# A two-layer block with experts: the loop for left-over tokens at the end, the first weights' loads, and the read of the record table

## The chip, the cores and the metric

The kernel runs on one core of a Trainium2 chip. The metric is the device time of one execution in microseconds (us). TensorE does the matrix products, VectorE (DVE), ScalarE (ACT) and GpSimd (POOL) the rest; DMA transfers are issued from the queues of SP, ScalarE and GpSimd.

## The reference, cut to what matters

There are 512 image tokens and 256 context tokens of 1024 numbers each. In both layers a mixer (three kinds of attention, joined by a gated product and `w_out`) is added to the tokens. Layer 0 does this for all 768 tokens, layer 1 for the 512 of the image alone. Then each token goes to two of 16 experts.

```python
for l in range(DEPTH):                                   # two layers
    h = rms_norm(x, g_norm1[l]) * (1.0 + sc1) + sh1
    y, yc = mixer_sublayer(h, hc, ...)
    x = x + gt1 * y
    h = rms_norm(x, g_norm2[l]) * (1.0 + sc2) + sh2
    ...
    scores = jax.nn.sigmoid(tokens @ w_router)           # 16 experts, the best two are used
    hid = jax.nn.silu(xb @ w_gate[e]) * (xb @ w_up[e])   # 1024 -> 512, for the tokens of expert e
    y = hid @ w_down[e]                                  # 512 -> 1024
    x = x + gt2 * out[:b * length].reshape(x.shape)
return rms_norm(x, g_final)
```

The scale and shift vectors (`sc1`, `sh1`, `gt1`, `sc2`, `sh2`, `gt2`) come from products of a condition vector with `w_mod`.

## The kernel before

**Weights.** All weights are read once, in a fixed order, in chunks of 512 KB (128 partitions of 1024 numbers), by SP's queue (`Weights.load`, L83). A load is written into the program as soon as a page of memory is free for it by the program's own count, up to a bound `ws.limit`, after which the loads wait until the bound is raised. A chunk is used raw, or it is split in two halves of its precision: ScalarE makes `wh` (L102), DVE makes `wl` (L114), and each product is three matmuls.

**Out phase.** `out_phase` multiplies the joined branches by `w_out`, one tile of 128 tokens after the other, six in layer 0 and four in layer 1. While TensorE is in tile m, the steps of the norm and the routing of tile m−1 or m−2 are hooked in between its products (`HOOKS`, `second`). The last tile has a class of its own (`Last`); its `end` stores the normed rows `h` for the gathers (L1539) and the tokens (L1540), both on SP's queue, and then raises the bound for the weights. The bound is 20 chunks into the experts' weights from the start of the phase, and 28 from there on. The pages of `w_out` come free during the last tile.

**Routing.** `Router.pair` works on two tiles at a time. TensorE gives the ranks of the tokens in their experts (`rk`), DVE compares (`oh`) and makes a row number for each place, and TensorE multiplies the comparisons with the tokens' numbers (`first`, L2168) so that the first 128 tokens of the experts 13, 14 and 15 are known at once. The last pair starts the gather of the first expert's rows (`x0`, L2173) as soon as its numbers are there. Then four indirect stores write records of token and weight to a table in memory (L2204). `finish` reads the table's part for these three experts on ScalarE's queue (`rec`, L2217), and `arrange` orders the other 13 experts.

**Experts.** `moe` works through 16 slots. The first three are the experts 13 to 15, whose weights (36 chunks) can be loaded before the routing is done; the experts of the 13 others are read by SP from the order table. A slot gathers its tokens' rows from memory, multiplies by gate, up and down, and its `finish` scatters the result with GpSimd (L1669), in layer 1 by adding to the tokens. Later slots use raw weights for 64 tokens.

**The loop.** Slots have a fixed number of places. Tokens above it are worked off in a hardware loop (`For_i`, L1949) over `nmore` rounds, a number that the routing gives; its body is `late_block`. It stands behind slot 10 in layer 0 and behind slot 13 in layer 1 (`LOOPAT`). All five engines read `nmore` and branch there.

**What follows the experts.** In layer 0 there come three groups of modulation products for layer 1 (`fillers`, matmuls into `modps`), and then the mixer of layer 1: it loads a tile of the tokens and of the experts' result (L623, L625), adds and norms them, and transposes them (`h1t`, L648). In layer 1 the final gain is loaded (`gf`, L1971), the four tiles of the tokens are read back (`cx`, L1975), normed and stored (L1979).

Of the kernel before, what the change touches and what calls it, by code (L numbers as in the profile page):

```python
# [10 lines left out]
BF16 = mybir.dt.bfloat16  # L11
I32 = mybir.dt.int32
AF = mybir.ActivationFunctionType
OP = mybir.AluOpType
# [4 lines left out]
NE = 16  # L19
# [4 lines left out]
PG1 = 14  # L24
MW = 8
EX = {0: 3, 1: 5}
LB = 1
RING = 10


# [122 lines left out]
def tile_dit(ctx, tc, a, out):  # L153
    nc = tc.nc
# [47 lines left out]
    h2d = {l: dram.tile([(6 - 2 * l) * 128, D], F32, name=f"h2d{l}") for l in range(2)}  # L202
# [56 lines left out]
    last_out = {}  # L259
# [73 lines left out]
    ws = Weights(nc, specs)  # L333
# [144 lines left out]
    def mod_row(pool, tag, l, j, v, name):  # L478
        t = pool.tile([128, D], F32, tag=tag, name=name)
        nc.sync.dma_start(t, bc(modd[l][j, v, :], D))  # L480
        return t
# [853 lines left out]
    def merge(l):  # L1335
# [4 lines left out]
        rt = st.enter_context(tc.tile_pool(name=f"rt{l}", bufs=1))  # L1340
# [87 lines left out]
        R = Router(tc, nc, rt, small, l, nm, tri, ones, br, oac_tile, tabd[l], h2d[l])  # L1428
# [13 lines left out]
        last = nm - 1  # L1442
# [33 lines left out]
        class Last:  # L1476
# [57 lines left out]
            def end(self):  # L1534
                j = 1 if last >= NIMG else 0
                self.norm()
                self.turn(1)
                nc.vector.scalar_tensor_tensor(self.h, self.u, self.r[:, 0:1], sh2[j], op0=OP.mult, op1=OP.add)
                nc.sync.dma_start(h2d[l][last * 128:(last + 1) * 128, :], self.h)  # L1539
                nc.sync.dma_start(xa[l][last], xo[last])  # L1540
                ws.limit = last_out[l] + NEXT[l]
                ws.load()
                self.score(1)
                s = sg_of(last)
                nc.vector.scalar_tensor_tensor(s, self.lo[:, 0:NE], self.r[:, 0:1], self.shw, op0=OP.mult, op1=OP.add)
                nc.scalar.activation(s, s, AF.Sigmoid)
# [14 lines left out]
        def out_phase():  # L1561
# [6 lines left out]
            mod_rows(0)  # L1568
            load_x(0)
            load_x(1)  # L1570
            ws.limit = last_out[l] + FIRST[l]
            ws.load()
            steps = {}

# [52 lines left out]
            x0 = pool0.tile([128, D], F32, tag="pg", name=f"x0{l}")  # L1627
# [11 lines left out]
    def moe(l, R, late, ex, x0):  # L1639
# [217 lines left out]
        def next_fetch():  # L1857
            if queue:
                queue.pop(0).fetch()
# [11 lines left out]
        ws.low()  # L1871
        for _ in range(XG[l]):
            next_fetch()
        ws.limit = first_in + NEAR if l == 0 else len(ws.specs)
        ws.load()
        for s in range(AHEAD, NE):
# [46 lines left out]
        for s in range(NE):  # L1923
            nx = s + 1 < NE
            if nx:
                for b in blocks[s + 1]:
                    b.turn()
                    ahead()
            up = products(s, "u")
            gate(s, 0, 4, up, lambda i: blocks[s][i].times(up[i]))  # L1930
            if nx:
                gp = products(s + 1, "g")
                gate(s + 1, 0, HIDAT, gp)
            for b in blocks[s]:
                b.hidden()
            if nx:
                gate(s + 1, HIDAT, 4, gp)
                silus(s + 1, gp)
            for b in blocks[s]:
                b.sums()  # L1940
            for k in range(4):
                chunk(blocks[s], k, lambda i, c, w: blocks[s][i].down(*w, c))
            if l == 0 and not nx:
                ws.pump(4 * len(TURN) + WEND)
            ws.low()
            for b in blocks[s]:
                b.finish()
            if s == LOOPAT[l]:
                with tc.For_i(0, nc.values_load(R.nmore[0:1, 0:1], min_val=0, max_val=SLOTS)) as j:  # L1949
                    late_block(j)  # L1950
            if l == 0 and s == NE - 2:
                for j in range(2):
                    gt2.append(mod_row(pool0, "pg", 0, j, 5, f"gt2{j}"))
        if l == 0:
            for _ in fillers(TURN, pool0, "pg", held):
                pass
# [35 lines left out]
AHEAD = 3  # L1992
# [2 lines left out]
HT = {0: 2, 1: 1}  # L1995
TROWS = 896
MORE = 6
LOOPAT = {0: 10, 1: 13}
YO = {0: 2, 1: 1}
XG = {0: 2, 1: 1}  # L2000
NS = NE - AHEAD
SLOTS = 14
# [7 lines left out]
MPG = 4  # L2010
HIDAT = 2
YT = (0, 2)
HOOKS = {(0, 0): 1, (0, 4): 1, (0, 5): 2, (1, 1): 1, (1, 5): 1, (1, 7): 1}
LEAD = 3
FIRST = {0: 20, 1: 20}
NEXT = {0: 28, 1: 28}


def of_kind(l, kind):
# [18 lines left out]
class Router:  # L2038
# [77 lines left out]
    def pair(self, m, s, x0=None):  # L2116
# [42 lines left out]

        f = w[:, 15, :, 0:AHEAD]  # L2160
        stt(f, r2[:, :, NS:NE], 1.0, bb[:, :, NS:NE], op0=OP.add, op1=OP.mult)
        psf = self.oac_tile(f"first{l}_{m}")
        shape = [128, 2, 128]
        for e in range(AHEAD):
            oh = rt.tile(shape, BF16, tag="oh", name=f"oh{l}_{m}{e}", bufs=2)
            tt(oh, self.places[:, None, :].to_broadcast(shape), f[:, :, e:e + 1].to_broadcast(shape), op=OP.is_equal)
            for i in range(4):
                nc.tensor.matmul(psf[:, e:e + 1], oh[:, i // 2, :], self.idc[:, i % 2, m + i // 2:m + i // 2 + 1],  # L2168
                                 start=i == 0, stop=i == 3)
            if x0 is not None:  # L2170
                tt(self.first[:, e:e + 1], self.firstf[:, e:e + 1], psf[:, e:e + 1], op=OP.add)
                if e == 0:
                    nc.gpsimd.indirect_dma_start(  # L2173
                        out=x0, out_offset=None, in_=self.h2d,
                        in_offset=bass.IndirectOffsetOnAxis(ap=self.first[:, 0:1], axis=0))

                    tt(self.cum[:, m + 1, :], bb[:, 0, :], bb[:, 1, :], op=OP.add)
                    tt(self.cum[:, m + 2, :], self.cum[:, m, :], self.cum[:, m + 1, :], op=OP.add)
        if x0 is None:
            tt(self.firstf, self.firstf, psf[:, 0:AHEAD], op=OP.add)  # L2180
            tt(self.cum[:, m + 1, :], bb[:, 0, :], bb[:, 1, :], op=OP.add)
            tt(self.cum[:, m + 2, :], self.cum[:, m, :], self.cum[:, m + 1, :], op=OP.add)
        row = w[:, 14]
        stt(row, r2, float(NE), self.eidx[:, None, :].to_broadcast([128, 2, NE]), op0=OP.mult, op1=OP.add)
        four = [128, 2, 2, NE]
# [15 lines left out]
        for j in range(2):  # L2201
            for k in range(2):
                nc.gpsimd.memset(self.spacer, 0.0)
                st = nc.gpsimd.indirect_dma_start(  # L2204
                    out=self.tabd, out_offset=bass.IndirectOffsetOnAxis(ap=self.idx[:, m + j, k:k + 1], axis=0),
                    in_=self.recs[:, m + j, k, :], in_offset=None)
                for o in self.scat:
                    self.tc.declare_no_dep(st.ins, o.ins, reason="each record has a row of its own")
                self.scat.append(st)
        yield  # L2210

    def finish(self):

        nc, nt = self.nc, self.nt
        ps = self.oac_tile(f"cnt{self.l}")
        nc.tensor.matmul(ps[:, 0:NE], self.ones, self.cum[:, nt, :], start=True, stop=True)
        nc.scalar.dma_start(self.rec.rearrange("p e f -> p (e f)"),  # L2217
                            self.tabd.rearrange("(s e) f -> s (e f)", e=NE)[0:128, 4 * NS:4 * NE])
        self.arrange(ps[:, 0:NE])

    def record(self, out, at):
        self.nc.gpsimd.indirect_dma_start(
# [181 lines left out]
```

## Time and profile before

| | |
|---|---|
| time, median of 3 runs | 3008.33 us (3006.95 to 3015.96) |
| the profiled execution | 3013.33 us |
| its span | 3011.5 us |
| granted clock of TensorE, mean | 0.963 |
| TensorE busy | 2788.7 us, 93% |
| VectorE, ScalarE, GpSimd busy | 61%, 42%, 12% |
| DMA, mean over the span | 185 GB/s |

A share is an average over stages that differ. The page's 40 slices show it for DMA: its busy share is two or three tenths in the attention of both layers and nine tenths or more in three slices of each expert stage.

### The profile page before, as it was taken

What the parts mean: (1) busy time and instruction counts of PE and PEld (TensorE: products, weight loads), DVE (VectorE), ACT (ScalarE), POOL (GpSimd) and SP (SyncE); (2) the same over time, 40 slices, a digit from 0 to 9 for tenths busy, and PEclk for the clock granted to TensorE, in tenths of its full rate; (3) what the DMA queues carried; (4) which work ended last, traced back from release to release, by engine and by line L of the source; (5) the groups of instructions that cost most, each with busy time, mean ns of one, the idle gap of its engine ahead of it and who ended that gap; (6) DMA issues with size and microseconds to landing.
All of it is one profiled execution on the core that took longest, in us unless ns stands there. A gap on an engine that the chain in (4) does not pass through costs nothing. (4 is left out here: it accounts for less than half of the span.)

```text
span 3011.5 us, 42058 instructions
## 1 busy us (share of the span) xinstructions
PE 2788.7 (93%) x15253; PEld 2235.7 (74%) x15253; DVE 1822.4 (61%) x3235; ACT 1279.0 (42%) x2376; POOL 363.3 (12%) x425
## 2 busy tenths in 40 slices
PE   7999999999999999969999699999999999969983
PEld 4788888888888667757766478878888877757651
DVE  4675567676554455658665666667775645657441
ACT  4444445455443211227655454444554442226330
POOL 1220000000011000022221231000000100022211
PEclk8999999999999999979999899999999999979996
DMA  6333222222333666669998732232234456769995
GB/s 237 130 110 101 88 76 95 87 81 87 130 131 105 238 252 240 238 218 341 347 362 292 251 115 95 74 105 69 93 103 140 149 198 232 270 218 380 369 376 183
DMA packets 203989, 557.63 MB, mean 185 GB/s; under 512 B 27238, under 2 KB 51942, under 8 KB 203776
## 3 DMA queue, kind: packets, MB, share of 16 engines
q1 hardware_dynamic: 175968, 503.64, 46.6%
q0 software_dynamic: 10688, 25.02, 3.4%
q10 hardware_dynamic: 17120, 26.23, 2.4%
q8 instruction: 121, 1.98, 0.3%
q14 instruction: 92, 0.75, 0.1%
HBM read 461.95 MB, written 96.77 MB: 186 GB/s over the span
## 5 line engine op out<-in xcount | busy, mean ns | idle before, releaser
L114 DVE TENSOR_TENSOR wl<-raw,wh 128x1024 fp32r<-128x1024 f32 x474 | 565.2, 1221 | 150.5 <-ACT wh L102 140.3
L102 ACT CAST wh<-raw 128x1024 fp32r<-128x1024 f32 x474 | 484.7, 1050 | 365.4 <-DMA raw<-oT 122.1
L892 ACT ACTIVATE P<-sc,st 128x768 f32<-128x768 f32 (+4 forms) x240 | 176.2, 734 | 340.5 <-DVE st L890 213.9
L890 DVE TENSOR_REDUCE st<-sc 128x1 f32<-128x768 f32 (+4 forms) x240 | 178.6, 744 | 118.9 <-PE sc L179 113.3
L179 PE MATMUL psb<-wl,wh 128*128 128x512 f32 x480 | 189.7, 395 | 6.9 <-DVE wl L114 6.6
L926 ACT CAST ptH<-pt 128x512 fp32r<-128x512 f32 x264 | 142.9, 591 | 124.1 <-PE pt L911 103.6
L179 PE MATMUL psb<-wh,wh 128*128 128x512 f32 x480 | 192.9, 402 | 1.5 <-ACT wh L102 1.5
L179 PE MATMUL psb<-wh,wl 128*128 128x512 f32 x480 | 189.1, 394 | 2.0 <-DVE wl L114 2.0
L936 DVE TENSOR_TENSOR ptL<-pt,ptH 128x512 fp32r<-128x512 f32 x264 | 169.6, 682 | 9.3 <-ACT ptH L926 7.3
L911 PE MATMUL pt<-ident,P 128*128 128x128 f32 x1056 | 141.4, 275 | 14.2 <-ACT P L892 11.3
L911 PEld LDWEIGHTS pt<-ident,P 128*128 128x128 f32 x1056 | 119.7, 140 | 44.8 <-ACT P L892 31.0
L179 PE MATMUL psR<-wh,hH 128*128 128x512 f32 (+1 forms) x384 | 150.7, 392 | 0.0
L179 PE MATMUL psR<-wl,hH 128*128 128x512 f32 (+1 forms) x384 | 147.2, 383 | 2.7 <-DVE wl L114 2.7
L179 PE MATMUL psR<-wh,hL 128*128 128x512 f32 (+1 forms) x384 | 147.6, 384 | 0.0
L898 DVE TENSOR_SCALAR P<-P,st 128x768 f32<-128x768 f32 (+3 forms) x240 | 130.0, 542 | 8.5
L179 PEld LDWEIGHTS psb<-wh,wh 128*128 128x128 f32 x480 | 90.9, 189 | 46.8 <-issue 18.7
L486 POOL TENSOR_SCALAR rstd<-ss 128x4 f32<-128x4 f32 (+2 forms) x70 | 21.6, 309 | 830.6 <-ACT h L492 359.6
L179 PEld LDWEIGHTS psb<-wl,wh 128*128 128x128 f32 x480 | 91.1, 190 | 28.4 <-DVE wl L114 10.8
L179 PE MATMUL sc<-swkT,swqs 128*128 128x256 f32 x704 | 109.1, 281 | 2.2 <-ACT P L892 2.2
L179 PEld LDWEIGHTS psb<-wh,wl 128*128 128x128 f32 x480 | 91.0, 190 | 23.2 <-DVE wl L114 4.0
L179 PE MATMUL yps<-wh,hidT 128*128 128x512 f32 x320 | 105.0, 399 | 0.0
L1099 DVE COPY sc<-sink 128x1 f32<-128x1 f32 x160 | 25.8, 161 | 128.7 <-PE sc L179 122.5
(529 smaller groups left out, 6937.6 us busy)
## 6 DMA issues: line engine op xcount, KB each, us to landing
raw<-in_w_in_dram SPq DMA_DIRECT2D x136, 512.0 KB
raw<-in_w_gate_dram SPq DMA_DIRECT2D x128, 512.0 KB
raw<-in_w_up_dram SPq DMA_DIRECT2D x128, 512.0 KB
raw<-in_w_down_dram SPq DMA_DIRECT2D x128, 512.0 KB
raw<-in_w_mod_dram SPq DMA_DIRECT2D x96, 512.0 KB
raw<-in_w_br_dram SPq DMA_DIRECT2D x48, 512.0 KB
raw<-oT SPq DMA_DIRECT2D x30, 512.0 KB
raw<-in_w_out_dram SPq DMA_DIRECT2D x16, 512.0 KB
```

The source lines that it names most:

```text
L102: self.nc.scalar.copy(c.h, c.raw)
L114: self.nc.vector.tensor_tensor(c.l, c.raw, c.h.bitcast(F32), op=OP.subtract)
L179: nc.tensor.matmul(ps, lhs, rhs, start=start, stop=stop, skip_group_check=share)
L486: nc.gpsimd.tensor_scalar(r[:, 0:cnt], ss, four / n, four * EPS, op0=OP.mult, op1=OP.add)
L890: nc.vector.reduce_max(st[:, 1, h:h + 1], s[:, 0:self.ns], axis=AX.X, negate=True)
L892: nc.scalar.activation(self.P[h][:, 0:self.ns], s[:, 0:self.ns], AF.Exp, bias=st[:, 1, h:h + 1], accum_out=st[:, 2, h:h + 1])
L898: nc.vector.tensor_scalar(self.P[h][:, 0:self.nk], self.P[h][:, 0:self.nk], st[:, 3, h:h + 1], None, op0=OP.mult)
L911: nc.tensor.transpose(pt[:, c * 256 + h * 128:c * 256 + (h + 1) * 128], self.P[2 * x + h][:, i * 128:(i + 1) * 128], ident)
L926: nc.scalar.copy(ph, src)
L936: nc.vector.tensor_tensor(pl, src, ph.bitcast(F32), op=OP.subtract)
L1099: nc.vector.tensor_copy(s[:, nk:nk + 1], sink[:, hd:hd + 1])
```

## The change

There are four parts.

- The loop stands behind the last slot in both layers, before the modulation products in layer 0 and before the final gain's load in layer 1. `LB`, the number of buffers of tiles in the loop's body, is 2 instead of 1.
- The bound on weight loads is 36 chunks from the start of the out phase; it is not raised in `Last.end`. The store of the last tile's `h` goes by ScalarE's queue.
- The read of the record table leaves `finish` and becomes `R.load`, issued from GpSimd's queue after the first gathers of the experts' rows.
- In `pair`, for all but the last pair, the comparisons are done in the old place and the products `first` with their sum are moved behind the record stores, into a step of their own; `HOOKS` has one more entry for it. In the last pair the sum over the counts (`add_up`) comes behind the three products. `oh` is one tile of three instead of three from two buffers.

```diff
-LB = 1
+LB = 2
...
                 nc.vector.scalar_tensor_tensor(self.h, self.u, self.r[:, 0:1], sh2[j], op0=OP.mult, op1=OP.add)
-                nc.sync.dma_start(h2d[l][last * 128:(last + 1) * 128, :], self.h)
+                nc.scalar.dma_start(h2d[l][last * 128:(last + 1) * 128, :], self.h)
                 nc.sync.dma_start(xa[l][last], xo[last])
-                ws.limit = last_out[l] + NEXT[l]
-                ws.load()
...
-            ws.limit = last_out[l] + FIRST[l]
+            ws.limit = last_out[l] + 12 * AHEAD
             ws.load()
...
         for _ in range(XG[l]):
             next_fetch()
+        R.load()
         ws.limit = first_in + NEAR if l == 0 else len(ws.specs)
...
-            if s == LOOPAT[l]:
-                with tc.For_i(0, nc.values_load(R.nmore[0:1, 0:1], min_val=0, max_val=SLOTS)) as j:
-                    late_block(j)
             if l == 0 and s == NE - 2:
                 for j in range(2):
                     gt2.append(mod_row(pool0, "pg", 0, j, 5, f"gt2{j}"))
+        with tc.For_i(0, nc.values_load(R.nmore[0:1, 0:1], min_val=0, max_val=SLOTS)) as j:
+            late_block(j)
         if l == 0:
             for _ in fillers(TURN, pool0, "pg", held):
...
-LOOPAT = {0: 10, 1: 13}
...
-HOOKS = {(0, 0): 1, (0, 4): 1, (0, 5): 2, (1, 1): 1, (1, 5): 1, (1, 7): 1}
+HOOKS = {(0, 0): 1, (0, 4): 1, (0, 5): 2, (1, 1): 1, (1, 3): 2, (1, 5): 1, (1, 7): 1}
...
-FIRST = {0: 20, 1: 20}
-NEXT = {0: 28, 1: 28}
...
-        psf = self.oac_tile(f"first{l}_{m}")
...
+        oh = rt.tile([128, AHEAD, 2, 128], BF16, tag="oh", name=f"oh{l}_{m}")
+
+        def places(e):
+            tt(oh[:, e], self.places[:, None, :].to_broadcast(shape), f[:, :, e:e + 1].to_broadcast(shape), op=OP.is_equal)
+
+        def numbers(e):
             for i in range(4):
...
+        if x0 is None:
+            for e in range(AHEAD):
+                places(e)
+            add_up()
+        else:
+            psf = self.oac_tile(f"first{l}_{m}")
+            for e in range(AHEAD):
+                places(e)
+                numbers(e)
...
+            add_up()
...
+        if x0 is None:
+            yield
+            psf = self.oac_tile(f"first{l}_{m}")
+            for e in range(AHEAD):
+                numbers(e)
+            tt(self.firstf, self.firstf, psf[:, 0:AHEAD], op=OP.add)
         yield
...
-        nc.scalar.dma_start(self.rec.rearrange("p e f -> p (e f)"),
-                            self.tabd.rearrange("(s e) f -> s (e f)", e=NE)[0:128, 4 * NS:4 * NE])
         self.arrange(ps[:, 0:NE])
+
+    def load(self):
+
+        self.nc.gpsimd.dma_start(self.rec.rearrange("p e f -> p (e f)"),
+                                 self.tabd.rearrange("(s e) f -> s (e f)", e=NE)[0:128, 4 * NS:4 * NE])
```

## Rows read from the trace of the kernel before

In the order of time `SPq` is SP's queue of DMA issues, and the bracket gives the idle time ahead of an instruction and what ended it.

**Rows 1.** The page: busy us (share of the span) and instructions of each engine.

```profile
PE 2788.7 (93%) x15253; PEld 2235.7 (74%) x15253; DVE 1822.4 (61%) x3235; ACT 1279.0 (42%) x2376; POOL 363.3 (12%) x425
```

**Rows 2.** Stretches: length, busy us (instructions) per engine, clock, DMA share, GB/s.

```profile
1275.00:1282.00 7.00, 6.72 (x34) 5.41 (x35) 4.07 (x16) 0.07 (x1) 2.90 (x5) 0.61 0.46 150
1576.00:1588.00 12.00, 0.45 (x3) 0.45 (x3) 0.00 (x0) 1.11 (x1) 1.62 (x1) 0.70 0.68 237
1588.00:1660.00 72.00, 72.00 (x386) 50.94 (x386) 45.98 (x45) 44.01 (x50) 8.96 (x7) 0.98 0.88 310
2760.00:2939.00 179.00, 166.62 (x967) 103.79 (x965) 85.72 (x93) 64.65 (x81) 42.86 (x30) 0.96 1.03 373
2939.00:2965.00 26.00, 0.20 (x2) 0.21 (x3) 1.38 (x2) 0.00 (x0) 1.56 (x1) 0.57 0.78 294
```

**Rows 3.** Line 1949, the loop: instruction, count, duration in ns, first and last start.

```profile
L1949 SPq COMPARE_BRANCH  x6: 33/38/57, 1573.8 to 2965.3; - x6
```

**Rows 4.** Order of time, TensorE, around slot 10 of layer 0: start, us, instruction.

```profile
1587.56 1.97 PE L498 MATMUL xbt<-ident,xg 128*128 128x128 f32 x8 [11.55 <-issue]
```

**Rows 5.** Order of time, TensorE, end of layer 0.

```profile
1677.31 1.92 PE L179 MATMUL modps<-raw,sc 128*32 128x512 f32 x16
1683.73 5.04 PE L179 MATMUL modps<-raw,sc 128*32 128x512 f32 x32 [4.50 <-ACT yo L1791]
1698.86 1.97 PE L648 MATMUL h1t<-ident,n110ot 128*128 128x128 f32 x8 [10.10 <-ACT n110ot L642]
```

**Rows 6.** Order of time, SP's queue, end of layer 0.

```profile
1687.98 0.35 SPq L623 DMA_DIRECT2D n110kv<-xa  x1
1689.18 0.35 SPq L625 DMA_DIRECT2D n110ot<-yd  x1
```

**Rows 7.** Order of time, TensorE, behind slot 13 of layer 1.

```profile
2964.80 1.11 PE L1745 MATMUL xst<-ident,xg 64*128 64x64 f32 x8 [25.95 <-SPq L1949]
```

**Rows 8.** Order of time, SP's queue, slots 13 to 15 of layer 1.

```profile
2949.93 4.13 SPq L83 DMA_DIRECT2D raw<-in_w_down_dram  x4
2965.50 0.35 SPq L1971 DMA_DIRECT2D gf<-in_g_final_dram  x1
```

**Rows 9.** Chain of waits at the end: start, us, what.

```profile
2983.96 3.68 PE ysm L179 x16
...
2987.66 0.74 DVE yo L1795
...
2989.45 3.69 DMA xa<-yo,rows
...
2994.49 6.98 DMA cx<-xa
```

**Rows 10.** Order of time, SP's queue, routing of layer 1.

```profile
2678.46 0.33 SPq L1539 DMA_DIRECT2D h2d<-h  x1
...
2679.35 3.01 SPq L83 DMA_DIRECT2D raw<-in_w_gate_dram  x4
...
2699.44 9.27 SPq L83 DMA_DIRECT2D raw<-in_w_up_dram  x4
```

**Rows 11.** Order of time, TensorE, routing of layer 1.

```profile
2672.99 0.39 PE L179 MATMUL pso<-wh,yL 128*128 128x512 f32 x1
...
2694.13 1.97 PE L498 MATMUL xbt<-ident,x 128*128 128x128 f32 x8 [7.57 <-DMA x<-h2d,first]
2699.12 0.79 PE L179 MATMUL g<-wh,xH 128*128 128x512 f32 x1 [3.02 <-ACT xH L187]
```

**Rows 12.** Order of time, GpSimd, routing of layer 1.

```profile
2684.64 1.25 POOL L2173 DMA_INDIRECT x<-h2d,first  x1 [7.83 <-DVE cum L2177]
```

**Rows 13.** Order of time, ScalarE, routing of layer 1.

```profile
2697.11 1.04 ACT L102 CAST wh<-raw 128x1024 fp32r<-128x1024 f32 x1 [17.90 <-DMA tabd<-recs,ridx]
```

**Rows 14.** Order of time, TensorE, the counting products of layer 0.

```profile
1275.03 0.60 PE L2168 MATMUL first<-idc,oh 128*128 128x1 bf16 x8 [4.00 <-DVE oh L2166]
...
1310.26 0.59 PE L2168 MATMUL first<-idc,oh 128*128 128x1 bf16 x8 [3.68 <-DVE oh L2166]
```

More of the change, by code (lines that the diff above doesn't have):

```diff
@@ L2161, in pair, with add_up @@
         stt(f, r2[:, :, NS:NE], 1.0, bb[:, :, NS:NE], op0=OP.add, op1=OP.mult)
-        psf = self.oac_tile(f"first{l}_{m}")
         shape = [128, 2, 128]
-        for e in range(AHEAD):
-            oh = rt.tile(shape, BF16, tag="oh", name=f"oh{l}_{m}{e}", bufs=2)
-            tt(oh, self.places[:, None, :].to_broadcast(shape), f[:, :, e:e + 1].to_broadcast(shape), op=OP.is_equal)
+        oh = rt.tile([128, AHEAD, 2, 128], BF16, tag="oh", name=f"oh{l}_{m}")
+        def places(e):
+            tt(oh[:, e], self.places[:, None, :].to_broadcast(shape), f[:, :, e:e + 1].to_broadcast(shape), op=OP.is_equal)
+        def numbers(e):
             for i in range(4):
-                nc.tensor.matmul(psf[:, e:e + 1], oh[:, i // 2, :], self.idc[:, i % 2, m + i // 2:m + i // 2 + 1],
+                nc.tensor.matmul(psf[:, e:e + 1], oh[:, e, i // 2, :], self.idc[:, i % 2, m + i // 2:m + i // 2 + 1],
                                  start=i == 0, stop=i == 3)
-            if x0 is not None:
+        def add_up():
+            tt(self.cum[:, m + 1, :], bb[:, 0, :], bb[:, 1, :], op=OP.add)
+            tt(self.cum[:, m + 2, :], self.cum[:, m, :], self.cum[:, m + 1, :], op=OP.add)
+        if x0 is None:
[7 more added lines that the diff above has]
+                numbers(e)
                 tt(self.first[:, e:e + 1], self.firstf[:, e:e + 1], psf[:, e:e + 1], op=OP.add)
@@ L2175, in pair @@
                         in_offset=bass.IndirectOffsetOnAxis(ap=self.first[:, 0:1], axis=0))
[L2177 to L2182, printed above, removed]
+            add_up()
         row = w[:, 14]
```

## The prediction

> **What bounds the kernel now.** I read the page's busy shares first, then the stretches, then what stands around each pause of TensorE. TensorE works 2788.7 of the span's 3011.5 us [rows 1], so most of the program cannot be shortened by moving waits; what an edit of this kind can win is in the 200-odd us in which TensorE stands, and in what a pause costs afterwards in clock. The reader is to see two different regimes. In the expert stage of layer 0 TensorE works without a break right after the pause of the token loop (1588 to 1660: 72.00 of 72.00 busy) while DMA has room (0.88). In layer 1 DMA is full (1.03 from 2760 to 2939) and TensorE has gaps: there the weight stream, and no engine, sets the pace. Inside the loop's own stretches (1576 to 1588, 2939 to 2965) TensorE does 0.45 and 0.20 us of work, and the granted clock, 0.98 in the steady work between, falls to 0.70 and 0.57 [rows 2].
>
> The chance that the loop does work is excluded first: its line has 6 branches on SP for two loops, and no instruction of its body is in the trace [rows 3]. It runs zero times; its price is that all engines meet there and that SP first sees its loads land.
>
> **The change part by part.** Durations are of the profiled execution, 3013.33 us, 5.0 above the median of 3008.33. I apply the sum to the median.
>
> *Loop out of the middle, layer 0.* TensorE resumes at 1587.56 after a gap of 11.55 [rows 4]. Right behind it TensorE is busy without a break, so the whole gap is its loss. It resumes at half clock: 0.98 granted over 72 us is 1.4 lost [rows 2]. Loads do not take the gap over: the stage stays at 0.88 of DMA with TensorE full. Gain 13.0; bounds 11.5 (the clock lost elsewhere anyway) and 13.0.
>
> *Loop at the end, layer 0.* Now the pause stands after the last slot. Before, TensorE does a third of the next layer's modulation products there (1677.31, 1.92 us), waits 4.50 for ScalarE's yo, and does the rest (1683.73, 5.04 us); then it stands 10.10 us for the first tile of layer 1 [rows 5]. That tile's loads leave SP at 1687.98 and 1689.18, the second as soon as the last scatter of layer 0 has landed [rows 6]. With the join, nothing of it may start before that scatter lands (just before 1689.18) plus about 1 for the branch, so 1690.3; then all 48 products, 6.96 by the two rows, of which five sixths must be done before the tile's first load can go (it left 0.8 before their end), so 1696.5 instead of 1688.0: 8.5 later, and all of layer 1 with it. The bounds are 0 (the 4.50 and 10.10 already spent absorb it) and 13.0 (nothing absorbed). I take +8.5, as it follows from the rows in order.
>
> *Loop out of the middle and to the end, layer 1.* TensorE resumes at 2964.80, after 25.95 idle [rows 7]. SP reaches the loop only after the last of its weight loads, four issued from 2949.93 on in 4.13 us, and then sees them all land; its next issue, the final gain, is at 2965.50 [rows 8]. So the last weights lie in memory at about 2964, and behind that TensorE still has 22.8 us (2964.80 to the end of the last product at 2987.64 [rows 7, 9]). Without the pause this work runs beside the stream, and it is less than the stream takes for the same chunks (22.8 against the 26 of the pause). Only the last chunk's work stays behind the last landing, a quarter of the 3.68 us of the last 16 products, about 0.9. With the stream where it was, the end would be 2963.7 + 0.9 + 0.7 (one more scatter in the full stretch, my estimate) = 2965.3: gain 22.3.
>
> *The stream itself comes earlier.* SP stands for the last tile's h store until 2678.46, and only then issues eight weight loads, four from 2679.35 and four more behind [rows 10]. Their pages hold the out weights that TensorE reads for this tile, the last of them at 2672.99 [rows 11]. With the limit at 36 from the start and the store on ScalarE's queue, they go as these are read, about 10 us earlier, and no longer lie just ahead of the x gather at 2684.64 [rows 12], which takes 9.5 us until TensorE has its rows (2694.13 [rows 11]), where a lone scatter lands in 3.69 [rows 9]. Next, ScalarE: its queue stands behind the record table's read, so that the weight's cast comes at 2697.11 after 17.90 idle, one cast (1.04) ahead of the xH copy which TensorE waits for, 3.02 [rows 11, 13]. On GpSimd's queue the read stops nobody but the next fetch. The copy itself waits for the scatters of the same memory, as the fetch behind them does, so I count only that cast and half a us of quicker landing: 1.6, in layer 0 on TensorE's path (bounds 0 and 3.4, the whole gap with its clock); in layer 1 the same chain frees the pages for the rest of the stream (2699.44 [rows 10]). There the burst starts 1.6 earlier for the chain and about 2 for the loads already gone: stream 3.7 earlier (bounds 0 and 6). With this the last product ends near 2961.6 instead of 2987.64: gain 26.0.
>
> *What is late next.* The tail: behind the last yo (2987.66) come a scatter 3.69, four row loads whose last takes 6.98, and the norm [rows 9]. The loop now stands between scatter and loads (+1.2), and the final gain's 512 KB, so far loaded beside TensorE's work, goes ahead of the row loads: its share of a burst of five is a fifth or more of 6.98, +1.7. Together +2.9 (bounds 1 and 4.5).
>
> *The routing pair.* The products that count the first places make TensorE wait for DVE's comparisons, 4.00 us in layer 0's fourth tile and 3.68 in its last; layer 1 has one like the latter [rows 14]. Now the comparisons are done a step ahead, and TensorE meets only h's transposes. In the fourth tile that leaves 0.7 us of wait; 3.3 go, and the 2.7 lost behind it at 0.61 of the clock over 7 us [rows 2]: 6.0 (bounds 3.3 and 7). In the other two, the shift rows follow closely and need a small PSUM tile that DVE's row step must first release (two buffers, one held by the ranks): that wait ends nearly where the old one did. I take 1.4 each (bounds 0 and 3.7).
>
> **The sum.** 13.0 − 8.5 + 6.0 + 1.4 + 1.4 + 1.6 + 26.0 − 2.9 = 38.0 us. By the median: 3008.3 − 38.0 = 2970.3, near 2970.
>
> A rule of the Trainium skill speaks against the earlier gather: by "DMA: Bandwidth & Descriptors", section "Queues, rings and completion order", an engine takes turns between the queues that have work, so that GpSimd's gather would not wait behind SP's loads. By it the half us of quicker landing, and with it about one of the stream's 3.7, would go, and the sum would be 36.5. The trace's 9.5 against 3.69 us rather shows a share taken by the loads, though the two move different sizes.
>
> **Rivals.**
> *A. The end of layer 0 gives back all that its middle gains.* That is so when the first tile's chain behind the join also meets the low clock and the modulation's own steps on DVE, 4.5 more. Then 13.0 in place of 8.5, sum 33.5: 2975. For it: TensorE idles from 1677 to 1699 nearly in one piece. Against: the 48 products are all that stands in between.
> *B. The stream doesn't move; this part of the change does nothing.* The eight pages come free only with the last product, or the thirteen register reads of SP behind set the burst. Then 3.7 and 1.6 go, sum 32.7: 2976. For it: in layer 1 DMA has no room after 2760. Against: between 2678 and 2700 it does.
> *C. The end of layer 0 is free, and the pairs gain their gaps wholly.* 8.5 and twice 2.3 more, sum 51.1: 2957. For it: 14.6 us of waiting there already. Against: the loads' order on SP.
> *D. Only part of layer 1's pause is won.* TensorE, now starved by the stream chunk by chunk, works at 0.57 of the clock as in the pause, so that the last slots fall behind it: up to half of 22.8 stays behind the landings, +11, sum 27.0: 2981. For it: the clock there. Against: 26 us are there for it.
> *E. Slower.* The pause at the end of layer 0 exposes the whole change of layers: beside it so far run the loads of layer 1's first weights, and if SP meets the loop with them unissued, none comes until after the join, and DVE, ScalarE and TensorE stand for them. Each load that slips behind the join costs the 1.4 us that its 512 KB take at the 373 GB/s of the full stretch [rows 2]; from 46.5 us (the sum and the 8.5 in it), 33 chunks, it makes the kernel slower, and with 40 it takes 3018. Against: only two to four loads are issued there.
>
> **How the numbers follow.** Chances: forecast 0.48, A 0.15, B 0.13, C 0.09, D 0.10, E 0.03; the last 0.02 is that everything is made up by a lower clock elsewhere and the time stays. The likeliest is 2970. Bounds of the terms, taken all to one side, give 2950 and 2989; I take 2956 to 2985, which holds A, B, C and D and leaves out E. About 0.3% (9 us) is what a measurement of this kernel can tell from no change; all cases but the last two are beyond it: faster 0.95, same 0.02, slower 0.03.
>
> **What would show it.** Right: TensorE without a gap near slot 10 of layer 0; a gap of some 13 us before the modulation products at its end, with the first tile's transposes about 20 us behind it; in layer 1, last product within 2 us of the last weight's landing, no gap of 26, and the branch between the last scatter and the row loads; the eight weight loads issued before the x gather; no gap of 4.00 in the fourth tile, one of 3 to 4 at the shift rows. Wrong: casts in layer 0 that wait for loads after the removed pause; a product tail of 10 us and more behind the last landing; a gap at layer 0's end beyond 20 us.

## The result, and the profile after

The changed kernel takes 2964.12 us (median of 4; 2957.83 to 2966.29), the kernel before 3012.14 beside it: a ratio of 0.9837 [0.9811, 0.9863], 49 us faster by that ratio. The forecast was 2970, 38 faster than the 3008.33 that it starts from. A second measurement of the same program (e9) gave 0.9835 [0.9821, 0.9848], 49.7 us by the medians. The forecast's 38 us are a ratio of 0.9874, outside both intervals, so that a gain beyond the forecast is no accident of one run; its 11 us are known to a few us only. The profiled execution is the fastest of its four (2957.83), which makes the pair of traces differ by 55.5 us; the profile of e9 (2964.01) is nearer to the median, and both are used below.

The page after, busy time of each engine:

```profile
PE 2770.4 (94%) x15253; PEld 2221.1 (75%) x15253; DVE 1820.3 (62%) x3235; ACT 1279.6 (43%) x2376; POOL 366.2 (12%) x427
```

TensorE is busy 18.3 us less than before [rows 1], for the same number of products: that part goes with the clock (mean granted 0.975, before 0.963), and some of it lies where nothing was changed (953.7 against 957.3 us busy over the first 1000 us). The rest of the 55.5 is idle time that went. The stretches after (length, busy us and instructions of each engine, then clock, DMA share, GB/s), in the order of [rows 2]:

```profile
1267.00:1274.00 7.00, 6.29 (x36) 4.92 (x35) 5.88 (x12) 2.50 (x4) 0.77 (x3) 1.00 0.31 126
1561.00:1632.00 71.00, 71.00 (x390) 50.10 (x388) 46.38 (x45) 44.39 (x52) 12.15 (x9) 1.00 0.98 352
1648.00:1660.00 12.00, 0.00 (x0) 0.00 (x0) 2.45 (x2) 2.68 (x3) 1.82 (x1) 0.71 0.36 94
2726.00:2904.00 178.00, 165.93 (x977) 104.40 (x976) 85.96 (x93) 64.39 (x81) 41.94 (x30) 0.97 1.03 372
2904.00:2930.60 26.60, 21.31 (x136) 8.51 (x134) 3.38 (x6) 1.72 (x4) 3.13 (x2) 1.00 0.82 301
```

The 7 us at the place of the fourth tile's counting products run at 1.00 of the clock instead of 0.61, and so do the 7 behind its gap of 0.71 (1272.4 to 1279.4). The stretch behind slot 10 has 1.00 instead of 0.98. The pause now stands from 1648 to 1660, with no product in 12 us and a clock of 0.71. The stream of layer 1 has what it had, 1.03 of DMA. And in its last 26.6 us TensorE does 21.31 us of work, where it did 0.20 of 26.

TensorE in order of time after, at the places of [rows 4, 5, 7, 11] (start, us, instruction, idle time ahead and what ended it):

```profile
1272.45 1.06 PE L498 MATMUL h2t<-ident,h 128*128 128x128 f32 x8 [0.71 <-DVE rw L2156]
...
1559.67 1.04 PE L498 MATMUL xbt<-ident,xg 128*128 128x128 f32 x8
...
1660.44 6.72 PE L179 MATMUL modps<-raw,sc 128*32 128x512 f32 x48 [12.63 <-DMA mb<-in_b_mod_dram]
1677.20 1.97 PE L648 MATMUL h1t<-ident,n110ot 128*128 128x128 f32 x8 [10.04 <-ACT n110ot L642]
...
2662.76 1.97 PE L498 MATMUL xbt<-ident,x 128*128 128x128 f32 x8 [6.82 <-DMA x<-h2d,first]
2665.95 0.80 PE L179 MATMUL g<-wh,xH 128*128 128x512 f32 x1 [1.22 <-ACT xH L187]
...
2903.53 0.71 PE L1743 MATMUL xst<-ident,xg 64*128 64x64 f32 x8
...
2929.52 1.08 PE L179 MATMUL ysm<-raw,hidS 128*64 128x512 f32 x4
```

The transposes at 1559.67 and 2903.53 have no idle time ahead of them: both pauses are gone from there. In their place stands one of 12.63 ahead of the modulation products, with the same 10 us behind it. In the routing, the wait for x is hardly shorter (6.82, before 7.57), the one for the copy is (1.22, before 3.02).

SP's queue after, at the places of [rows 6, 8, 10]:

```profile
1666.38 0.35 SPq L623 DMA_DIRECT2D n110kv<-xa  x1
1666.77 0.43 SPq L625 DMA_DIRECT2D n110ot<-yd  x1
...
2634.56 5.29 SPq L83 DMA_DIRECT2D raw<-in_w_gate_dram  x4
2641.07 3.89 SPq L83 DMA_DIRECT2D raw<-in_w_down_dram  x4
2645.92 8.97 SPq L83 DMA_DIRECT2D raw<-in_w_up_dram  x2
2654.98 1.73 SPq L1540 DMA_DIRECT2D xa<-xo  x1
...
2915.15 4.15 SPq L83 DMA_DIRECT2D raw<-in_w_down_dram  x4
2937.14 0.35 SPq L1969 DMA_DIRECT2D gf<-in_g_final_dram  x1
```

The first tile's loads leave 18.6 us after the end of the last expert product (1647.81, before 10.6). The eight loads that stood behind the token store now leave from 2634.56 to 2645 and ahead of it (2654.98). The final gain goes out behind the loop, at 2937.14, just ahead of the row loads; the last of these takes 6.16 us in the chain of waits (before 6.98):

```profile
2938.01 6.16 DMA cx<-xa
```

ScalarE in the routing of layer 1 ([rows 13]):

```profile
2663.11 1.05 ACT L102 CAST wh<-raw 128x1024 fp32r<-128x1024 f32 x1 [14.52 <-DMA xa<-xo]
2664.88 1.01 ACT L187 CAST xH<-xbt 128x1024 fp32r<-128x1024 f32 x1 [0.72 <-PE xbt L498]
```

The copy (xH) follows the transposes of x at once; the cast is ahead of it and in nobody's way.

The same instruction's start in two traces, taken at points between the edits, shows where the time went. Each line is the change of that shift over its stretch (before's times), in us:

| stretch of before | what it holds | forecast | after | e9 |
|---|---|---|---|---|
| 0 to 1268 | nothing changed | 0 | −2.1 | +0.9 |
| 1268 to 1301 | counting products, fourth tile | −6.0 | −5.8 | −5.9 |
| 1301 to 1335 | counting products, last tile | −1.4 | −5.6 | −3.7 |
| 1335 to 1364 | routing, layer 0 | −1.6 | −2.6 | −1.5 |
| 1570 to 1600 | pause at slot 10 gone | −13.0 | −13.4 | −13.4 |
| 1660 to 1740 | pause at the end of layer 0 | +8.5 | +8.1 | +9.5 |
| 1740 to 2640 | mixer of layer 1 | 0 | −3.7 | −3.6 |
| 2640 to 2683 | counting products, layer 1 | −1.4 | −5.5 | −5.6 |
| 2683 to 2935 | routing and stream, layer 1 | −3.7 | −4.6 | −5.5 |
| 2935 to 2984 | pause at slot 13 gone | −22.3 | −22.1 | −22.4 |
| 2984 to the end | tail | +2.9 | +1.9 | +1.8 |
| sum | | −38.0 | −55.5 | −49.3 |

The forecast's 26.0 for layer 1 stands in two lines, 3.7 and 22.3. Long unchanged stretches differ between executions by 3 us (first line) and, in the mixer of layer 1, by up to 8 over all the runs below. Short lines at an edit agree better: that of the fourth tile is −5.8 or −5.9 in every run that has the change there.

### The profile page after: what moved, and what is told of

It is laid out like the page before. It is cut to its first block, busy times and chain, and to the rows that moved or that the text cites. A ratio compares the mean times of both kernels' runs of the same rounds, so it can differ in the third digit from the quotient of the medians.

```text
span 2956.0 us, 42080 instructions
## 1 busy us (share of the span) xinstructions
PE 2770.4 (94%) x15253; PEld 2221.1 (75%) x15253; DVE 1820.3 (62%) x3235; ACT 1279.6 (43%) x2376; POOL 366.2 (12%) x427
## 5 line engine op out<-in xcount | busy, mean ns | idle before, releaser
L911 PE MATMUL pt<-ident,P 128*128 128x128 f32 x1056 | 141.4, 275 | 14.7 <-ACT P L892 11.8
```

The source lines that it names most:

```text
L911: nc.tensor.transpose(pt[:, c * 256 + h * 128:c * 256 + (h + 1) * 128], self.P[2 * x + h][:, i * 128:(i + 1) * 128], ident)
```

## The experiments

The theory from here on (theory 1): the pauses came as forecast; what is beyond it is the counting products of the two last tiles, which gain their whole gap and the clock behind it, 5 to 6 us each and not 1.4. The rival: the surplus is from the loop or from the weights' loads.

**One part alone, in the kernel before.** Four kernels, each with one part of the change.

e1, the loop:

```diff
-LB = 1
+LB = 2
...
-            if s == LOOPAT[l]:
-                with tc.For_i(0, nc.values_load(R.nmore[0:1, 0:1], ...)) as j:
-                    late_block(j)
...
+        with tc.For_i(0, nc.values_load(R.nmore[0:1, 0:1], ...)) as j:
+            late_block(j)
```

> The kernel before with nothing but the loop behind the last slot in both layers. Theory 1 (the loop's parts came as forecast): layer 0 gains the 13 us of the pause at slot 10 and pays about 7 at its end; layer 1 gains about 22, the work behind the pause, and pays 2 in the tail: 26 us faster, in the trace no gap over 2 us near slot 10, one of 11 to 13 ahead of the modulation products, the last product within 2 us behind the last weight. Rival (the surplus over the forecast comes from the loop): 35 us or more, with the stream of layer 1 ending earlier than 2960 or an end of layer 0 that costs under 3.

Measured: 0.9918 [0.9904, 0.9932], 25 us. By the shifts: −13.4 at slot 10, +8.2 to 1740, −22.4 at slot 13, +3.4 in the tail. The loop's terms came as forecast, and the surplus is not here.

e2, the pair step and its hook (the diff of the change from `f = w[:, 15...]` to the end of `pair`, and `HOOKS`):

```diff
-HOOKS = {(0, 0): 1, (0, 4): 1, (0, 5): 2, (1, 1): 1, (1, 5): 1, (1, 7): 1}
+HOOKS = {(0, 0): 1, (0, 4): 1, (0, 5): 2, (1, 1): 1, (1, 3): 2, (1, 5): 1, (1, 7): 1}
```

> The kernel before with nothing but the change in the pair step and its hook. Theory 1 (the counting products of both last tiles cost their whole gap and the half clock behind it, and no new wait comes in their place): 5 to 6 us each in three places, 16 in all; no gap over 1 us between the ranks and the shift rows. Rival (as forecast: the shift rows wait for the row step, 1.4 each in the two last tiles): 9 us, with a gap of about 3.5 at the second shift product. In layer 1 the gain lies ahead of the weight stream and moves its start, so it stays in the total.

Measured: 0.9943 [0.9928, 0.9958], 17 us; shifts −5.8, −4.0 and −6.9 in the three places. TensorE in the last tile of layer 0 of e2:

```profile
1302.10 0.55 PE L179 MATMUL shr<-wr,shcol 128*1 128x16 f32 x16
1302.99 0.36 PE L179 MATMUL shb<-shrow,onerow 1*128 1x16 f32 x2 [0.34 <-ACT shrow L1493]
...
1307.74 0.45 PE L2170 MATMUL first<-idc,oh 128*128 128x1 bf16 x12
```

The second shift product (`shb`) waits 0.34 us, and that for the row ahead of it on ScalarE. There is no wait of 3.5. The changed kernel itself shows why; first TensorE, then VectorE in the same stretch:

```profile
1299.38 0.55 PE L179 MATMUL shr<-wr,shcol 128*1 128x16 f32 x16
1300.27 0.36 PE L179 MATMUL shb<-shrow,onerow 1*128 1x16 f32 x2 [0.34 <-ACT shrow L1493]
...
1305.02 0.45 PE L2165 MATMUL first<-idc,oh 128*128 128x1 bf16 x12
```

```profile
1301.85 1.09 DVE L2161 TENSOR_TENSOR oh<-places,rw 128x256 bf16<-128x256 bf16 x3
...
1303.15 0.18 DVE L2188 SCALAR_TENSOR_TENSOR rw<-rk,eidx 128x32 f32<-128x32 f32 x1
```

The shift product runs at 1300.27, VectorE's row step, which I had it wait for, at 1303.15. It does not wait for the buffer that the ranks hold. The clock behind the gap is the other part of the gain. First before, the gap of layer 1 and the ten us behind that of layer 0's last tile (its 3.68 is in [rows 14]); then e2, ten us from the ranks on:

```profile
2656.47 0.60 PE L2168 MATMUL first<-idc,oh 128*128 128x1 bf16 x8 [3.69 <-DVE oh L2166]
...
1310.00:1320.00 10.00, 9.17 (x55) 7.03 (x56) 5.00 (x18) 1.77 (x6) 4.21 (x7) 0.66 1.00 377
```

```profile
1301.00:1311.00 10.00, 8.89 (x74) 6.82 (x73) 7.56 (x22) 3.17 (x8) 3.30 (x8) 1.00 0.98 349
```

In e2's ten us the 0.66 is gone. That the line of layer 0's last tile is 5.6 in the changed kernel's first trace and 3.7 in e9 goes with a stretch a little further on: e9 runs at 0.50 from 1312.5 to 1315.8, half of which is 1.7 us, the first trace at 1.00 from 1308 to 1315. Theory 1 holds, and the rival, which was my forecast, is out.

e3, the loads:

```diff
-                nc.sync.dma_start(h2d[l][last * 128:(last + 1) * 128, :], self.h)
+                nc.scalar.dma_start(h2d[l][last * 128:(last + 1) * 128, :], self.h)
                 nc.sync.dma_start(xa[l][last], xo[last])
-                ws.limit = last_out[l] + NEXT[l]
-                ws.load()
...
-            ws.limit = last_out[l] + FIRST[l]
+            ws.limit = last_out[l] + 12 * AHEAD
```

> The kernel before with nothing but the bound of 36 from the start and the last tile's h store on ScalarE's queue. Theory 1: eight loads leave about 10 us earlier in each layer, the x gather is quicker by 1 to 2 us, and the stream of layer 1 starts as much earlier: 2 to 4 us faster in all. Rival A (the surplus over the forecast is from here): 8 us or more. Rival B (the gather takes turns with the loads and doesn't wait for them): the time from the gather's issue to TensorE's transposes stays at 9.5 in layer 1, total 0 to 1.

Measured: 0.9981 [0.9972, 0.999], 6 us, more than the 2 to 4 expected and short of rival A's 8. TensorE, then ScalarE, in the routing of layer 1:

```profile
2687.27 1.97 PE L498 MATMUL xbt<-ident,x 128*128 128x128 f32 x8 [2.71 <-DMA x<-h2d,first]
2695.16 0.79 PE L179 MATMUL g<-wh,xH 128*128 128x512 f32 x1 [5.92 <-ACT xH L187]
```

```profile
2693.15 1.04 ACT L102 CAST wh<-raw 128x1024 fp32r<-128x1024 f32 x1 [15.93 <-DMA tabd<-recs,ridx]
2694.10 1.00 ACT L187 CAST xH<-xbt 128x1024 fp32r<-128x1024 f32 x1
```

The wait for x falls from 7.57 to 2.71, and from the gather's issue to the transposes it is 4.7 and 4.6 us in the two layers (before 8.5 and 9.5), though the h store leaves about as far ahead of it as before (6.6 and 6.2 us, before 5.8 and 6.2) and the token store nearer to it (0.9 and 1.2, before 5.4 and 5.8). So it is the loads that made the difference, and rival B is out. But the next wait grows from 3.02 to 5.92: ScalarE stands behind the record table's read until 2693.15, so of 4.9 us two arrive. The routing gains 1.1 and 2.0 us, the stream behind it 1.4.

e4, the record table's read:

```diff
-        nc.scalar.dma_start(self.rec.rearrange("p e f -> p (e f)"),
-                            self.tabd.rearrange("(s e) f -> s (e f)", e=NE)[0:128, 4 * NS:4 * NE])
...
         for _ in range(XG[l]):
             next_fetch()
+        R.load()
```

> The kernel before with nothing but the record table's read on GpSimd's queue. Theory 1: ScalarE's cast leaves ahead of the x copy, the first product of the experts comes about 1.6 us sooner in layer 0, and in layer 1 the gap of 3.02 ahead of it falls to about 1.2: 2 to 3 us in all, below what the time can tell; the gaps tell it. Rival (the copy waits for the scatters of the same memory anyway): the gaps of 3.41 and 3.02 stay, 0 us.

Measured: 0.9986 [0.9977, 0.9995], 4 us, a little more than expected. ScalarE, then TensorE, in layer 1:

```profile
2681.33 1.05 ACT L102 CAST wh<-raw 128x1024 fp32r<-128x1024 f32 x1 [3.89 <-DMA xa<-xo]
2694.88 1.01 ACT L187 CAST xH<-xbt 128x1024 fp32r<-128x1024 f32 x1 [12.51 <-DMA tabd<-recs,ridx]
```

```profile
2692.11 1.97 PE L498 MATMUL xbt<-ident,x 128*128 128x128 f32 x8 [7.32 <-DMA x<-h2d,first]
2695.95 0.79 PE L179 MATMUL g<-wh,xH 128*128 128x512 f32 x1 [1.86 <-ACT xH L187]
```

The cast leaves early (2681.33), and the gap ahead of the first product falls to 1.86 in layer 1; but ScalarE's idle time ahead of the copy ends with the landing of the records, 0.8 us after the transposes (2692.11 and 1.97, so 2694.08), so that the rival is half right: in layer 0 that gap stays at 3.93, and nothing is gained there. Layer 1 gains 1.4 in the routing and 1.4 in the stream. The four parts make 0.0172 in all, the change 0.0163 and 0.0165: they add up within their intervals.

**One part undone, in the changed kernel.** e5 puts the loop of layer 0 back behind slot 10:

```diff
+            if l == 0 and s == 10:
+                with tc.For_i(0, ...) as j:
+                    late_block(j)
...
-        with tc.For_i(0, ...) as j:
-            late_block(j)
+        if l == 1:
+            with tc.For_i(0, ...) as j:
+                late_block(j)
```

> The changed kernel with the loop of layer 0 back behind slot 10, that of layer 1 at the end. Theory 1 (the move in layer 0 is worth 13 gained less 7 paid): 6 us slower than the changed kernel. Rival A (the end of layer 0 pays as much as the middle gains): the same time. Rival C (the end is free): 13 slower.

Measured: 0.9856 [0.9841, 0.9871] against the change's 0.9837: 6 us slower, though the intervals meet. With no pause at its end, the stretch from 1660 to 1740 costs 1.6 us over before's trace, so the pause there is worth 6.5 to 8 of the 8.1 and 9.5. (e2, e3 and e4, with no loop there either, have 1.1 to 1.8 in that line, so the trace of before is on the short side.) Rival A of the prediction is out, and so is the free end of rival C; its other half, pairs that gain their gaps wholly, is what e2 showed.

e6 puts the record read back on ScalarE's queue, behind the counting:

```diff
-        R.load()
...
+        nc.scalar.dma_start(self.rec.rearrange("p e f -> p (e f)"),
+                            self.tabd.rearrange("(s e) f -> s (e f)", e=NE)[0:128, 4 * NS:4 * NE])
         self.arrange(ps[:, 0:NE])
```

> The changed kernel with the record table's read back on ScalarE's queue, right behind the counting. Theory 1: the gap ahead of the first product of the experts is 3 again instead of 1.2 in both layers, the stream of layer 1 starts 1.5 to 2 later, 3 us slower in all. Rival (with the early loads the read finds its records sooner and hides): gaps of 1.2 to 2, under 1 us.

Measured: 0.9854 [0.9839, 0.9869]. The routing gains 0.3 and 1.6 us where the change gains 1.5 to 2.6 and 2.5 to 3.2, the stream 1.1 where it gains 2.1: 3 to 5 us, as theory 1 has it. The gaps, though, are the rival's: from the end of the transposes to the first product 2.2 and 1.4 us, not 3.

e10 puts the bound on the loads back at 20 and 28, but leaves the h store on ScalarE's queue:

```diff
                 nc.sync.dma_start(xa[l][last], xo[last])
+                ws.limit = last_out[l] + 28
+                ws.load()
...
-            ws.limit = last_out[l] + 12 * AHEAD
+            ws.limit = last_out[l] + 20
```

> The changed kernel with the bound on weight loads back at 20 and then 28 in the last tile's end; the h store stays on ScalarE's queue. Theory 1 (the eight loads just ahead of the x gather delay it): the gather's rows come 8.5 to 9.5 us after its issue again instead of 6.5 to 7.4, the first product of the experts comes 1 to 2 us later after the first counting product in each layer, 3 to 5 us slower in all. Rival (the queues take turns, the gather doesn't wait for the loads): 6.5 to 7.4 stays.

Measured: 0.9849 [0.9834, 0.9864] beside 0.9835 [0.9821, 0.9848] in the same rounds, 4 us. But the gather took 6.2 and 6.0 us, not 8.5: SP, no longer held by the h store, had sent most of the eight earlier, three and four loads were issued in the last 10 us. So this kernel did not rebuild the old state, and says nothing about the gather; e3 does.

**Versions beyond the change.** e7 has the loop of layer 0 behind the modulation products and their sums:

```diff
-        with tc.For_i(0, ...) as j:
-            late_block(j)
         if l == 0:
             for _ in fillers(TURN, pool0, "pg", held):
                 pass
+            while conts:
+                conts.pop(0)()
+        with tc.For_i(0, ...) as j:
+            late_block(j)
...
-            conts.pop(0)()
-            conts.pop(0)()
             n1_sum(0)
```

> The changed kernel with the loop of layer 0 behind the modulation products and their sums instead of ahead of them. Theory 1 (the join costs 7 because the 48 products, 6.7 us, stand between it and the first tile's loads): the products run in the wait for the last scatter, the loads leave about 3 us sooner, held up by VectorE's sums of nearly 10; 2 to 4 us faster than the changed kernel, read as the time from the last expert product to the first transposes of layer 1. Rival (what stands behind the join is the chain of loads, norm and transposes alone, and the products are hidden beside it): no change in that time.

Measured: 0.9828 [0.9815, 0.9842], 2 to 3 us ahead of the changed kernel, within the intervals. TensorE, then SP, at the end of layer 0 of e7:

```profile
1652.82 1.92 PE L179 MATMUL modps<-raw,sc 128*32 128x512 f32 x16
1659.28 6.42 PE L179 MATMUL modps<-raw,sc 128*32 128x512 f32 x32 [4.53 <-ACTq L1952]
1681.94 1.97 PE L648 MATMUL h1t<-ident,n110ot 128*128 128x128 f32 x8 [16.25 <-DMA n113kv<-xa]
```

```profile
1654.30 0.92 SPq L419 DMA_DIRECT2D mb<-in_b_mod_dram  x3
1669.75 0.37 SPq L623 DMA_DIRECT2D n110kv<-xa  x1
```

The products run early, but the loads leave 16.9 us after the last expert product instead of 18.6, and the transposes stand 29.1 after it instead of 29.4 (e9: 30.0). The gap ahead of them is 16.25 now. By the time to the first transposes, which was to tell it, the expectation of 2 to 4 fails. But this doesn't show that the products were no term of that wait, and the gain is there one tile later. VectorE, first in the changed kernel, then in e7: the last of the three sums over the modulation products, and the first addition for the second tile:

```profile
1673.88 2.84 DVE L439 TENSOR_TENSOR mb<-modps,mb 2x512 f32<-2x512 f32 x4
1676.65 1.20 DVE L630 TENSOR_TENSOR n111ot<-n111ot,gt 128x1024 f32<-128x1024 f32 x1
```

```profile
1666.45 2.84 DVE L439 TENSOR_TENSOR mb<-modps,mb 2x512 f32<-2x512 f32 x4
...
1677.79 1.23 DVE L630 TENSOR_TENSOR n111ot<-n111ot,gt 128x1024 f32<-128x1024 f32 x1 [0.23 <-DMA n111ot<-yd]
```

In e7 the sums have taken the place of the products: the loop comes behind them, they end at 1669.29, and the first load leaves 0.5 us later. Where the sums end sooner the first tile does come sooner: in e12 below they end 11.8 us after the last expert product (e7: 16.4), the loads leave at 12.3 and the transposes stand at 24.0. And in the changed kernel the last sum stands between the first two tiles; in e7 it does not. The second tile's additions begin 24.9 us after the last expert product instead of 28.8, its transposes stand 40.4 after it instead of 42.4 (e9: 43.6), and the stretch from 1660 to 1740 costs 6.3 us instead of 8.1 and 9.5. So the new order is worth about 2 to 3 us behind the first tile. Products and sums were not moved apart.

e8 and e11 are e7 with the final gain's load ahead of the loop of layer 1:

```diff
+        if l == 1:
+            gfs.append(pool0.tile([128, D], F32, tag="pg", name="gf"))
+            nc.sync.dma_start(gfs[0], bc(a["g_final"], D))
         with tc.For_i(0, ...) as j:
             late_block(j)
```

> As the run before it, and the final gain's load of layer 1 ahead of its loop. Theory 1 (the gain's 512 KB share the DMA engines with the four row loads of the tail): the time from the last product of layer 1 to the end falls by 1 to 2 us from 25.4. Rival (SP's order alone counts, 0.4 of issue): 0.4.

> The changed kernel itself, beside the two versions below on one chip, to compare them in the same rounds. Expected 0.984 of the kernel before, as measured.

> The changed kernel with the loop of layer 0 behind the modulation products and their sums, and the final gain's load ahead of the loop of layer 1, once more in the same rounds as the changed kernel. By the two traces it is 2 us shorter at the end of layer 0 and 2 in the tail: 4 us faster than the changed kernel, 0.982 to 0.983 of the kernel before. Rival (the two gains are the runs' own scatter): the same time, within 1 us in the traces' two stretches.

Measured: e8 0.9815 [0.9799, 0.9831]; e11 0.9814 [0.9801, 0.9828], median 2958.40, beside e9 2964.67 in the same rounds. SP in the tail of e11:

```profile
2925.68 0.34 SPq L1955 DMA_DIRECT2D gf<-in_g_final_dram  x1
2942.55 2.16 SPq L1975 DMA_DIRECT2D cx<-xa  x4
```

The gain's load lies ahead of the last products. From the last product to the end it is 23.1 and 23.2 us in e8 and e11, 25.4 and 25.3 in the changed kernel: 2.2 off, somewhat more than expected. At the end of layer 0 the first transposes stand where they did (29.2 and 29.5), the second tile's come earlier as in e7 (40.4 and 40.9), and the stretch from 1660 to 1740 costs 6.0 and 6.4 (e9: 9.5). This version is the fastest measured, 6 us ahead of the change by the medians; the two intervals overlap by a little (0.9821 to 0.9828), and the two stretches account for 5 of the 6.

e12 is e11 with one load less ahead of the gather:

```diff
-            ws.limit = last_out[l] + 12 * AHEAD
+            ws.limit = last_out[l] + (27, 29)[l]
```

> The version with both, and the bound of loads at 27 in layer 0 and 29 in layer 1, one less than the pages hold, so that neither the last load, which waits for its page until just before the x gather, nor the token store behind it on SP comes right ahead of the gather. Theory 1: the gather's rows come 4.6 us after its issue instead of 6.3 to 6.9, as in the kernel with the loads' change alone; the copy behind it then waits for the record stores, so that the first product of the experts gains 0.5 to 1.5 us in each layer, 1 to 3 us in all. Rival (it is the stores of h and tokens that the gather waits for): 6 us or more stay.

Measured: 0.9841 [0.9827, 0.9854], slower than e11. ScalarE, then TensorE, in the routing of layer 0 of e12:

```profile
1330.77 1.04 ACT L102 CAST wh<-raw 128x1024 fp32r<-128x1024 f32 x1 [9.16 <-DMA xa<-xo]
1340.13 1.01 ACT L187 CAST xH<-xbt 128x1024 fp32r<-128x1024 f32 x1 [8.32 <-DMA tabd<-recs,ridx]
```

```profile
1333.47 1.97 PE L499 MATMUL xbt<-ident,x 128*128 128x128 f32 x8 [4.51 <-DMA x<-h2d,first]
1341.20 0.79 PE L179 MATMUL g<-wh,xH 128*128 128x512 f32 x1 [5.75 <-ACT xH L187]
```

The gather did become quicker, 4.8 and 4.5 us (e11: 6.4 and 6.5, with one load 0.8 us ahead of it). But the copy waits until 1340.13 for the records to land, and the first product comes 14.9 us after the first counting product (e11: 12.1); in layer 1 12.4 (12.2). The last of the four record stores is issued 6.1 us behind the gather, as in e11 (6.0), but lands 4.9 us later instead of 2.1; why was not tried. At the end of layer 0 another 3 us go (1660 to 1740: +9.6, e11 +6.4), although the first transposes stand only 24.0 us after the last expert product there: an earlier first tile does not by itself shorten that stretch. The expected gain is a loss.

## Why the prediction was right, and where its size was off

The direction, the range and the larger terms held. The pause at slot 10: 13.0 forecast, 13.4 in both traces and in e1. The pause at slot 13: 22.3 against 22.1 to 22.4, as worked out from the last landing and the last quarter of products (0.9 forecast, 1.08 in the row at 2929.52); rival D, half clock for the last slots, is out (1.00 granted there), and rival E, a slower kernel, is out with the time. The end of layer 0: +8.5 against +8.1 and +9.5. Its order was read rightly, a gap of 12.63, the products, the loads, and the loads left 8.0 us later than before, 0.8 ahead of the end of the products, as the term had it. e7 moved the products away and hardly moved the first transposes, but there the sums stand ahead of the loads in their stead; so the trace agrees with the term's working, and no run shows it alone. Products and sums behind the loop are some 2 to 3 us of the amount (e7, e8, e11). The tail: +2.9 against +1.9 in the table, but 3.5 and 3.4 up to the issue of the last store (18.2 us after the last product before, 21.7 and 21.6 after). From there to the end of the span it is 3.7 us in some traces and 5.7 in others whatever the kernel: 5.7 in before, e1, e2, e3 and e6, 3.7 in the changed kernel's two and all the rest. So 2 us of the table's line are not of the change. Of the 3.5, the branch is 0.9 to 1.0 (the row loads go out 6.5 us after the last product in e8 and e11, 5.6 before), for which I had 1.2, and the gain's load about 2.2, for which I had 1.7.

The term that was mis-sized is that of the counting products in the two last tiles: "that wait ends nearly where the old one did. I take 1.4 each". It measured 3.7 to 5.6 and 5.5 to 5.6 in the changed kernel, 4.0 and 6.9 in e2, that is, most of the gap of 3.7 and the clock behind it, as in the fourth tile, where 3.3 for the gap and 2.7 for the clock gave 6.0 and the traces 5.8. The step that failed is the wait of the shift rows for a PSUM buffer; the trace shows none. Nor could the term's bounds, 0 to 3.7, hold the rest: they leave out the clock, which before's trace has at 0.66 behind the gap. Of the surplus, 6.5 to 8.3 us are from here, and about 1.8 from the routing and the stream together (7.0 to 7.2 against 5.3).

The routing terms came near the right sum for the wrong reason. I gave the cast ahead of the copy 1.04 and the quicker gather half a us. e3 shows the gather 4 to 5 us quicker, and that the copy's wait for the records takes most of that back: it gains 1.1 and 2.0 us. e4 shows that the cast alone is worth nothing in layer 0 and 1.4 in layer 1. All parts together give 1.5 to 2.6, and 2.5 to 3.2. In the changed kernel the gather is only 2 to 3 us quicker (6.2 to 7.4 us), but the records come sooner: the first record store leaves 1.7 to 2.4 us behind the gather and the last lands at about 8 (before 3.8; in e3 3.2 and 3.8, landing at 9.2 and 9.8), so that the copy follows the transposes at once. I had no term for that. Rival B, a stream that does not move, is out: it ends 4.6 to 5.5 earlier by routing and loads.

The rule of the Trainium skill that I weighed ("DMA: Bandwidth & Descriptors", section "Queues, rings and completion order") says that the engines take turns between queues. I drew from it that the gather would not wait behind SP's loads. The runs disagree with what I drew. With eight loads issued in the 5.3 us ahead, the rows are there 8.2 to 9.5 us after the issue (before, e1, e2, e4), with none in the 9 us ahead 4.5 to 4.8 (e3, e12), and with one load 0.8 us ahead 6.2 to 7.6 (the changed kernel and its versions). That the engines take turns may be so; the gather does not go free of the loads.

The mixer of layer 1 (1740 to 2640) is 3.6 us shorter in both traces of the changed kernel, with not one instruction changed in it. The other runs speak against its being of the change: the line is −0.6 to −1.4 in e1 to e4, +0.4, +1.1 and +0.4 in e5, e6 and e10, −3.4 in e7, +3.9 and +3.5 in e8 and e11, and +1.7 in e12, all with the same instructions there. It goes with the granted clock (1745 to 2600): 1.00 in the two traces of the changed kernel, 0.99 in before, e5, e6, e8 and e11. What stays open is the rest of the surplus, 1 to 3 us, which is less than the intervals can tell, and how the 6.5 to 8 us at the end of layer 0 divide between the products, the sums and the join.

## What to carry to other kernels

Price a point where all engines meet by the stage that it stands in: here the same empty loop cost 13.4 us in the middle of a stage bound by products, 22 where it held back work that a full weight stream would have covered, and 6.5 to 8 and about 1 where the engines had to drain anyway. Price a short wait of TensorE with the clock behind it: gaps of 3.7 and 4.0 us were worth 4 to 7. And before a wait is called replaced by another, look in the trace for the instruction that would have to wait.

## What the runs showed of the hardware that was not expected

The rows of an indirect gather of 512 KB are there 4.5 to 4.8 us after its issue, or 8.2 to 9.5 when eight loads of 512 KB were issued on another queue in the 5.3 us ahead of it; one such load 0.8 us ahead makes it 6.2 to 7.6. Behind a TensorE gap of 4.00 us the granted clock was 0.61 over the next 7 us, behind one of 0.71 us at the same place 1.00. From the issue of the last store to the end of the span, the 14 traces here have 3.7 or 5.7 us and nothing between, whatever the kernel.
